# A hybrid decoder trunk: modulation products held back in pairs two to six of each group by tokens

## The chip, the core and the metric

One core of a Trainium2 chip. Its engines work side by side, each through a queue of its own in order: TensorE (PE, with PEld for the loading of its weights), VectorE (DVE), ScalarE (ACT), GpSimd (POOL) and SyncE (SP), which here only issues DMAs. The time is that of one execution on the device in microseconds (us), the median of several runs. Lower is better.

## The reference

Two layers, 256 tokens, a model width of 2048, all in float32. The modulation is `mod = silu(c) @ w_mod[i] + b_mod[i]`: 6 x 2048 numbers per layer from one vector `c`, so 12 x 8192 KB of weights a layer for very little arithmetic.

```python
c_act = jax.nn.silu(c)
for i in range(DEPTH):                      # 2 layers
    mod = (c_act @ w_mod[i] + b_mod[i])[:, None, :]
    sh1, sc1, g1, sh2, sc2, g2 = jnp.split(mod, 6, axis=-1)
    h = rms_norm(x, norm1_g[i]) * (1.0 + sc1) + sh1
    y = retention_mixer(h, ...) if i == 0 else short_conv_mixer(h, ...)
    x = x + g1 * y
    h = rms_norm(x, norm2_g[i]) * (1.0 + sc2) + sh2
    a, b = jnp.split(h @ ffn_w_in[i], 2, axis=-1)      # 2048 -> 2 x 5632
    x = x + g2 * ((silu(a) * b) @ ffn_w_out[i])        # 5632 -> 2048
return rms_norm(x, final_g)
```

## The kernel before

**Weights.** All weights of the products lie in `w_all`, in the order of their use, in chunks of 128 x 2048 numbers (1 MB). A chunk holds 16 blocks of 128 x 128, and it is loaded by `fetch` into one of three buffers named raw. `prepare` then splits it in pieces of 128 x 1024: ACT copies a piece to `hi` in a rounded format (line 395), DVE makes `lo = raw - hi` (line 398), and PE multiplies with both. There are four buffers each for hi and lo, and `take` prepares two pieces (three in parts of the feed-forward) ahead of the one in use.

**Modulation.** `modulation(layer, which, j)` makes 128 numbers of `mod`. It loads 1 MB of `w_mod` into a raw buffer of the same three, multiplies it on DVE with `cb` (silu of `c` on all partitions) and sums along the row in one instruction (line 311, 128 x 2048), and POOL adds the bias. There are 192 of these. 32 are made at the start; the other 160 are in the list `todo` in the order of their need: gate 1, scale 2, shift 2 and gate 2 of layer 0, then all six parts of layer 1. The instruction of line 311 has a low priority (`MOD_PRIO`) where the scheduler orders DVE's queue.

**When a modulation begins.** Every product calls `paced(n)` with the blocks that it used. `plan_mod` says how many modulations are due after so many blocks, and `allowed` grows by 0.045 a block up to 2.0, so `paced` begins at most one in about 22 blocks, or two at once when none was begun for a while. A call with more than 64 blocks sets `allowed` to zero. `needed(layer, which)` begins all that a step needs and that are not yet begun. One such call is `needed(1, GT2)` in line 1273, between the convolution and the last feed-forward: it empties `todo`, because the buffer of `cb` is used for something else from there.

**Groups by tokens.** In the feed-forward's input, `gathered` computes 128 + 128 tokens by 1024 columns (512 of each half of the SwiGLU) over all 16 blocks of rows, taken as eight pairs of rows, one chunk each. In an ordinary pair, a chunk takes 24 matmuls. Some pairs are of the class `Seven`: seven products in place of eight (Strassen-Winograd, 21 matmuls), for which DVE makes differences of the weights (lines 384 to 390) besides the lo's. Layer 0 has two pairs of seven in a group, the fourth and the sixth; layer 1 has three. After the last pair of seven, `mixed_sums` empties four banks (lines 1121 to 1125); after the group, line 1163 empties the other four. The results are multiplied and, at the third pair of the next group, transposed by PE (line 1177). Layer 0 has four groups in the first part and six in the second, each part followed by the feed-forward's output. Layer 1's output uses `gathered` too, when no modulation is left.

PE's order is written out by hand. The other engines' order comes from a scheduler in the recording layer, at build time.

Of the kernel before, what the change touches and what calls it, by code (L numbers as in the profile page):

```python
# [40 lines left out]
FIRST_SEVEN, IN_SEVEN, OUT_SEVEN, TURNS_AT, BESIDE_CB, BESIDE_SUMS = (3, 5), (3, 4, 6), ((2, 4, 6), (2, 4, 6)), 2, 40, 48  # L41
FFN_TILES = 20, 24
STORE_AT, LOAD_AT = 0, 2
LEAD_RET, LEAD_CONV, LEAD_FFN, TURN_ROW = 6, 4, 4, 6
AHEAD = 2
MOD_LEAD = 64
# [203 lines left out]
def trunk(ctx: ExitStack, tc: tile.TileContext, x_in, c_in, pos_in, w_mod, cols_in, gain_in, tab_in, w_all, out):  # L250
# [55 lines left out]
    def modulation(layer, which, j):  # L306
        t = layer * 6 * KT + which * KT + j
        raw = mod_raw(t)
        total = tmp("msum", (P, 1), bufs=4)
        with tc.high_priority(offset=MOD_PRIO):  # L310
            nc.vector.scalar_tensor_tensor(raw, raw, 1.0, cb, op0=ALU.mult, op1=ALU.mult, accum_out=total)  # L311
        b = b_mod[:, t : t + 1]
        norm = 0 if which < SH2 else 1
        if which in (SC1, SC2):
            m = tmp("mcol", (P, 1), bufs=4)
            nc.gpsimd.tensor_scalar(m, total, b, 1.0, op0=ALU.add, op1=ALU.add)
            dst = mod_a[layer][norm][:, j : j + 1]
            nc.gpsimd.tensor_tensor(dst, m, gain[norm][layer][:, j : j + 1], op=ALU.mult)
        else:
            dst = (mod_s if which in (SH1, SH2) else mod_g)[layer][norm][:, j : j + 1]  # L320
            nc.gpsimd.tensor_tensor(dst, total, b, op=ALU.add)

    todo = []
# [3 lines left out]
    n_mod = len(todo)  # L327
# [1 line left out]
    first = RET_SPANS[0].n * FIRST_KS  # L329
    early = sum(g.n * len(g.ks) for g in RET_SPANS)  # L330
    plan_mod = [(early, 0), (1024, 18), (1984, 49), (5184, n_mod)]
    units, allowed = [0], [0.0]

    def paced(n):

        units[0] += n
        due = 0
        for (a, i), (b, j) in zip(plan_mod, plan_mod[1:]):
            if units[0] >= a:
                due = min(j, i + (units[0] - a) * (j - i) // (b - a))  # L340
        allowed[0] = min(allowed[0] + n * MOST, 2.0) if n <= 64 else 0.0
        while todo and n_mod - len(todo) < due and allowed[0] >= 1.0:
            allowed[0] -= 1.0
            modulation(*todo.pop())

# [57 lines left out]
    def take(group, k, col, width=P):  # L403

        assert order.pop() == (group, k, col, width)
        i = place[0] or 0
        if i == 0:
            if place[0] == 0:
                ready.pop(0)
            while len(ready) < 1 + ahead_now[0] * (units[0] >= first):  # L410
                n = len(ready)
                prepare()
                if len(ready) == n:
                    break
        place[0] = (i + width) % ready[0][2]
        return [t[:, i : i + width] for t in ready[0][:2]]
# [13 lines left out]
    def product(g, act, base=0, before=None, banks=None, last=True):  # L430

        fresh = not banks
        banks = banks or [bank() for _ in g.cols]
        for k in g.ks:
            if before:
                before(k)
            h = act[k - base]
            for c, pt in zip(g.cols, banks):
                hi, lo = take(g, k, c)
                nc.tensor.matmul(  # L440
                    pt, hi, h, start=fresh and k == g.ks[0], stop=False, skip_group_check=True
                )
                nc.tensor.matmul(  # L443
                    pt[:, 1, :], lo, h[:, 0, :], start=False, stop=last and k == g.ks[-1], skip_group_check=True
                )
            ticked(len(g.cols))
        paced(len(g.cols) * len(g.ks))
        return banks
# [11 lines left out]
    def by_token(banks, hi, lo, h, first, last, halves=range(2)):  # L460

        for t in halves:
            thrice(banks[t], half_of(h, t), (hi, lo), first, last)

    def packed(g, act, base=0, before=None, between=None, banks=None):

        banks = banks or [bank() for _ in range((g.n + 1) // 2)]  # L470
        for k in g.ks:
            if before:
                before(k)
            h = act[k - base]
            at = 0
            for i, (c, width) in enumerate(g.items):
                if between and i == len(g.items) // 2:
                    between(k)
                hi, lo = take(g, k, c, width)
                if width == DV:  # L480
                    both = [v.rearrange("p a b -> p (a b)") for v in banks[at // 2 : at // 2 + 2]]
                    by_token(both, hi, lo, h, k == g.ks[0], k == g.ks[-1])
                    at += 4
                    continue
                pt = banks[at // 2][:, at % 2, :]
                first, last = k == g.ks[0] and at % 2 == 0, k == g.ks[-1]
                nc.tensor.matmul(pt, hi, h[:, 0, :], start=first, stop=False, skip_group_check=True)  # L487
                nc.tensor.matmul(pt, hi, h[:, 1, :], start=False, stop=False, skip_group_check=True)  # L488
                nc.tensor.matmul(pt, lo, h[:, 0, :], start=False, stop=last, skip_group_check=True)  # L489
                at += 1  # L490
            ticked(g.n)
        paced(g.n * len(g.ks))
        return banks
# [103 lines left out]
    def normed(accs, layer, norm, g):  # L597
# [18 lines left out]
        for k in g.ks:  # L616
# [11 lines left out]
            elif k > SPREAD_AT:  # L628
                more(min(k, made[0] + 2))
        more(KT)  # L630
        paced(len(g.cols) * len(g.ks))

        def total(pt, dst=None):
# [38 lines left out]
    with ExitStack() as inner:  # L672
# [64 lines left out]
        with tc.tile_pool(name="start", bufs=1) as sp:  # L737
# [132 lines left out]
            due, step = [], [0.0]  # L870
# [229 lines left out]
    def flat_bank():  # L1100
        return bank().rearrange("p a b -> p (a b)")

    def sevens(g, act, base, sums, ours, banks, first, last):

        s1, s2, s4 = [[v[:, n, :] for n in range(2)] for v in sums]
        (a11, s3), (a12, a22) = [[half_of(act[k - base], t) for t in range(2)] for k in g.ks]
        p1, p5, p6, p7 = [(b, first, last) for b in banks]
        for use, x, (o, a, z) in zip(g.uses(), (s4, a12, s1, s3, a11, s2, a22), (
            (ours[0, 1], False, False), (ours[0, 0], False, False), p5, p7, p1, p6, (ours[1, 0], False, False)
        )):  # L1110
            thrice(o, x, take(*use), a, z)
            if use[2] in ("B21", "T3", "T2"):
                paced(4)
        paced(4)

    def mixed_sums(banks):

        p1, p5, p6, p7 = banks
        u1, u3 = halves_of
        u2, u4 = [tmp("u512", (P, DV), pool=mpool, bufs=3) for _ in range(2)]  # L1120
        nc.scalar.copy(u1, p1)
        nc.vector.tensor_tensor(u2, p6, u1, op=ALU.add)
        nc.vector.tensor_tensor(u3, p7, u2, op=ALU.add)
        nc.vector.tensor_tensor(u4, p5, u3, op=ALU.add)
        nc.vector.tensor_tensor(u2, p5, u2, op=ALU.add)
        return {(0, 0): u1, (1, 0): u3, (1, 1): u4, (0, 1): u2}
# [3 lines left out]
    def gathered(groups, act, base, sums, beside=None, mixed=None, single=None):  # L1130

        ours = {(t, j): flat_bank() for t in range(2) for j in range(2)}
        banks, n = [], len(sums)
        for i, g in enumerate(groups):
            if beside:
                beside(i)
            if i == TURNS_AT and waiting:
                waiting.pop(0)()
            if isinstance(g, Seven):
                n -= 1  # L1140
                banks = banks or [flat_bank() for _ in range(4)]
                of = sums[(g.ks[0] - base) // 2]
                sevens(g, act, base, of, ours, banks, n == len(sums) - 1, n == 0)
                if not n:
                    extra = mixed_sums(banks)
                    if mixed:
                        mixed(extra)
                continue
            if len(g.cols) == 1:
                single(g, ours, g is groups[-1])  # L1150
                continue
            for k in g.ks:
                for j, item in enumerate(g.items):
                    ends = i == 0 and k == g.ks[0], g is groups[-1] and k == g.ks[-1]
                    by_token([ours[t, j] for t in range(2)], *take(g, k, *item), act[k - base], *ends)
                paced(g.n)
        return ours, extra
# [241 lines left out]
    for part in range(2):  # L1399
# [10 lines left out]
        for i, groups in enumerate(LAST_IN[part]):  # L1410
            due = OUT_SEVEN[part]
# [42 lines left out]
```

## Time and profile before

| | us |
|---|---|
| median of 3 runs | 2627.31 |
| lowest and highest | 2624.63, 2629.22 |
| the profiled execution, its own time | 2629.53 |
| its span, first to last instruction | 2627.8 |
| PE busy in the span | 2570.7 (98%) |
| DVE busy | 2296.9 (87%) |
| line 311 (modulation), 160 instructions on DVE | 365.9 |
| line 398 (lo) on 128 x 1024 from raw, 912 instructions on DVE | 1104.0 |
| DMA, mean over the span | 262 GB/s |
| granted TensorE clock, mean | 0.998 |

In rows of the timeline, the first number is the start in us from the span's start, the second the duration, then come engine, line, operation, out<-in and shapes; the bracket at the end is the engine's idle time ahead of it, with what ended it. In rows of the stretches, each engine has its busy time and its instructions, then come the granted clock, the DMA engines' busy share and GB/s.

### The profile page before, as it was taken

What the parts mean: (1) busy time and instruction counts of PE and PEld (TensorE: products, weight loads), DVE (VectorE), ACT (ScalarE), POOL (GpSimd) and SP (SyncE); (2) the same over time, 40 slices, a digit from 0 to 9 for tenths busy, and PEclk for the clock granted to TensorE, in tenths of its full rate; (3) what the DMA queues carried; (4) which work ended last, traced back from release to release, by engine and by line L of the source; (5) the groups of instructions that cost most, each with busy time, mean ns of one, the idle gap of its engine ahead of it and who ended that gap; (6) DMA issues with size and microseconds to landing.
All of it is one profiled execution on the core that took longest, in us unless ns stands there. A gap on an engine that the chain in (4) does not pass through costs nothing.

```text
span 2627.8 us, 35162 instructions
## 1 busy us (share of the span) xinstructions
PE 2570.7 (98%) x13563; PEld 2197.6 (84%) x13563; DVE 2296.9 (87%) x2838; ACT 1312.3 (50%) x1726; POOL 140.6 (5%) x232
## 2 busy tenths in 40 slices
PE   7999999999999999999999999999999999999998
PEld 6898889888898777877778899888898888888886
DVE  7988978887799998889998889988988998999978
ACT  5544543444456444334444455444565564565554
POOL 0000000010000011100000000000000000000000
PEclk9999999999999999999999999999999999999999
DMA  9976668777686776877777777887755555555653
GB/s 399 385 289 225 253 253 303 280 268 265 255 305 230 293 293 258 297 291 292 268 290 273 282 297 286 323 302 291 286 194 192 207 208 209 184 213 180 222 211 145
DMA packets 96683, 689.48 MB, mean 262 GB/s; under 512 B 10737, under 2 KB 12161, under 8 KB 13441
## 3 DMA queue, kind: packets, MB, share of 16 engines
q1 hardware_dynamic: 96514, 687.23, 70.3%
q8 instruction: 106, 1.74, 0.3%
q14 instruction: 63, 0.52, 0.1%
HBM read 685.08 MB, written 2.11 MB: 262 GB/s over the span
## 4 chain that ended last, share of the span: by engine, by line
PE 76%; DVE 14%; DMA 6%; issue 3%; ACT 1%; ACTq 0%; DVEq 0%; POOLq 0%; POOL 0%; SPq 0%
PE bank L440 17%; PE bank L454 13%; PE bank L455 13%; PE bank L453 13%; PE bank L443 9%; DVE lo L398 6%; DMA raw<-w_all 5%; DVE raw L311 2%; PE bank L489 2%; PE bank L488 2%; PE bank L487 2%; PE bank L620 1%; PE bank L622 1%; PE bank L621 1%; DMA raw<-w_mod 1%
## 5 line engine op out<-in xcount | busy, mean ns | idle before, releaser
L395 ACT CAST hi<-raw 128x1024 fp32r<-128x1024 f32 (+1 forms) x974 | 984.7, 1024 | 1036.6 <-PE bank L455 347.6
L398 DVE TENSOR_TENSOR lo<-raw,hi 128x1024 fp32r<-128x1024 f32 (+1 forms) x974 | 1143.4, 1188 | 242.7 <-ACT hi L395 237.8
L454 PE MATMUL bank<-lo,h 128*128 128x512 f32 x1592 | 628.3, 395 | 23.3 <-DVE lo L398 22.8
L453 PE MATMUL bank<-hi,h 128*128 128x512 f32 x1592 | 626.4, 393 | 3.2 <-DVE rm L732 2.4
L455 PE MATMUL bank<-hi,h 128*128 128x512 f32 x1592 | 622.4, 391 | 0.0
L454 PEld LDWEIGHTS bank<-lo,h 128*128 128x128 f32 x1592 | 300.2, 189 | 101.0 <-DVE lo L398 43.0
L311 DVE SCALAR_TENSOR_TENSOR raw<-raw,cb 128x2048 f32<-128x2048 f32 x160 | 365.9, 2287 | 19.4 <-DMA raw<-w_mod 18.3
L453 PEld LDWEIGHTS bank<-hi,h 128*128 128x128 f32 x1592 | 300.1, 188 | 67.5 <-ACT hi L395 4.5
L455 PEld LDWEIGHTS bank<-hi,h 128*128 128x128 f32 x1592 | 300.0, 188 | 61.8
L440 PE MATMUL bank<-mid,hi 128*128 128x512 f32 x920 | 319.6, 391 | 0.2 <-ACT hi L395 0.2
L443 PE MATMUL bank<-mid,lo 128*128 128x256 f32 x920 | 259.6, 282 | 2.3 <-DVE lo L398 2.3
L440 PE MATMUL bank<-h,hi 128*128 128x512 f32 x736 | 255.4, 391 | 0.0
L443 PE MATMUL bank<-h,lo 128*128 128x256 f32 x736 | 207.4, 282 | 0.0
L440 PEld LDWEIGHTS bank<-mid,hi 128*128 128x128 f32 x920 | 172.6, 188 | 36.2 <-ACT hi L395 0.5
L443 PEld LDWEIGHTS bank<-mid,lo 128*128 128x128 f32 x920 | 174.1, 189 | 3.1 <-DVE lo L398 3.0
L440 PE MATMUL bank<-rm,hi 128*128 128x512 f32 x496 | 172.5, 391 | 0.0
L440 PEld LDWEIGHTS bank<-h,hi 128*128 128x128 f32 x736 | 138.1, 188 | 28.8
L489 PE MATMUL bank<-h,lo 128*128 128x256 f32 x512 | 146.3, 286 | 4.8 <-DVE lo L398 4.8
L487 PE MATMUL bank<-h,hi 128*128 128x256 f32 x512 | 145.6, 284 | 3.3 <-ACT h L776 3.3
L488 PE MATMUL bank<-h,hi 128*128 128x256 f32 x512 | 145.6, 284 | 0.7 <-DVE h L777 0.7
L443 PE MATMUL bank<-rm,lo 128*128 128x256 f32 x496 | 139.9, 282 | 0.0
L443 PEld LDWEIGHTS bank<-h,lo 128*128 128x128 f32 x736 | 139.3, 189 | 0.0
(273 smaller groups left out, 3430.2 us busy)
## 6 DMA issues: line engine op xcount, KB each, us to landing
raw<-w_all SPq DMA_DIRECT2D x456, 1024.0 KB, 4.9
raw<-w_mod SPq DMA_DIRECT2D x192, 1024.0 KB, 5.6
x<-x_in SPq DMA_DIRECT2D x4, 512.0 KB, 5.4
out<-xt SPq DMA_DIRECT2D x4, 512.0 KB, 3.0
decay<-tab_in SPq DMA_DIRECT2D x8, 128.0 KB, 2.3
x<-gate_row SPq DMA_DIRECT2D x2, 512.0 KB, 4.3
last_gain<-gain_in SPq DMA_DIRECT2D x1, 1024.0 KB, 7.2
cols<-cols_in SPq DMA_DIRECT2D x1, 152.0 KB, 8.7
```

Of the source, the lines that this page charges most:

```text
L311: nc.vector.scalar_tensor_tensor(raw, raw, 1.0, cb, op0=ALU.mult, op1=ALU.mult, accum_out=total)
L395: nc.scalar.copy(hi, raw)
L398: nc.vector.tensor_tensor(lo, raw, hi.bitcast(F32), op=ALU.subtract)
L440: nc.tensor.matmul(pt, hi, h, start=fresh and k == g.ks[0], stop=False, skip_group_check=True)
L443: nc.tensor.matmul(pt[:, 1, :], lo, h[:, 0, :], start=False, stop=last and k == g.ks[-1], skip_group_check=True)
L453: nc.tensor.matmul(o, hi, w_hi, start=first, stop=False)
L454: nc.tensor.matmul(o, hi, w_lo, start=False, stop=False)
L455: nc.tensor.matmul(o, lo, w_hi, start=False, stop=last)
L487: nc.tensor.matmul(pt, hi, h[:, 0, :], start=first, stop=False, skip_group_check=True)
L488: nc.tensor.matmul(pt, hi, h[:, 1, :], start=False, stop=False, skip_group_check=True)
L489: nc.tensor.matmul(pt, lo, h[:, 0, :], start=False, stop=last, skip_group_check=True)
L620: nc.tensor.matmul(pt, hi, high, start=k == 0, stop=False, skip_group_check=True)
```

## The change

`paced` begins no modulation while `hold[0]` is set, and `gathered` sets it for the pairs 1 to 5 of a group, counted from zero. `allowed` still grows in these pairs, up to its cap. At the seventh pair two modulations may begin at once, and `needed` is as it was.

```diff
+HELD = range(1, 6)
...
-    units, allowed = [0], [0.0]
+    units, allowed, hold = [0], [0.0], [False]
...
         allowed[0] = min(allowed[0] + n * MOST, 2.0) if n <= 64 else 0.0
-        while todo and n_mod - len(todo) < due and allowed[0] >= 1.0:
+        while todo and n_mod - len(todo) < due and allowed[0] >= 1.0 and not hold[0]:
             allowed[0] -= 1.0
             modulation(*todo.pop())
...
         for i, g in enumerate(groups):
             if beside:
                 beside(i)
+            hold[0] = i in HELD
             if i == TURNS_AT and waiting:
                 waiting.pop(0)()
```

PE's order is the same in both kernels. Lines from 44 on stand one or two lines later in the changed kernel (lo is line 399 there, the modulation 312). The order of the instructions on DVE, in the second group of layer 0's first part, from the last piece of the fourth pair (a pair of seven) to the sixth pair. Before:

```order
L398 TENSOR_TENSOR lo_8412<-raw_8335,hi_8411 128x512
L311 SCALAR_TENSOR_TENSOR raw_8401,msum_8403<-raw_8401,cb 128x2048
L398 TENSOR_TENSOR lo_8424<-raw_8421,hi_8423 128x1024
L398 TENSOR_TENSOR lo_8434<-raw_8421,hi_8433 128x1024
L384 TENSOR_TENSOR differences<-raw_8443 128x1024
L398 TENSOR_TENSOR lo_8447<-raw_8443,hi_8446 128x1024
```

In the changed kernel, at the same place:

```order
L399 TENSOR_TENSOR lo_8392<-raw_8320,hi_8391 128x512
L399 TENSOR_TENSOR lo_8404<-raw_8401,hi_8403 128x1024
L399 TENSOR_TENSOR lo_8414<-raw_8401,hi_8413 128x1024
L399 TENSOR_TENSOR lo_8427<-raw_8423,hi_8426 128x1024
L399 TENSOR_TENSOR lo_8434<-differences,hi_8433 128x1024
```

The modulation behind the pair of seven is gone, and the difference for the sixth pair is made earlier (ahead of these rows).

DVE again, from the seventh pair's second lo to the first two lo's of the next group, in the changed kernel. The operations on bank are those that empty the products of seven (lines 1123 to 1126) and the first of the group's other banks (line 1165):

```order
L399 TENSOR_TENSOR lo_8490<-raw_8477,hi_8489 128x1024
L1123 TENSOR_TENSOR u_1548_8508<-bank_8388,halves 128x512
L399 TENSOR_TENSOR lo_8502<-raw_8499,hi_8501 128x1024
L1124 TENSOR_TENSOR halves<-bank_8389,u_1548_8508 128x512
L399 TENSOR_TENSOR lo_8516<-raw_8499,hi_8515 128x1024
L1125 TENSOR_TENSOR u_1549_8509<-bank_8387,halves 128x512
L1126 TENSOR_TENSOR u_1548_8508<-bank_8387,u_1548_8508 128x512
L312 SCALAR_TENSOR_TENSOR raw_8531,msum_8533<-raw_8531,cb 128x2048
L312 SCALAR_TENSOR_TENSOR raw_8536,msum_8538<-raw_8536,cb 128x2048
L1165 TENSOR_TENSOR halves<-bank_8266,halves 128x512
L399 TENSOR_TENSOR lo_8544<-raw_8541,hi_8543 128x1024
L399 TENSOR_TENSOR lo_8560<-raw_8541,hi_8559 128x1024
```

Before, one modulation stands between the lo's of the seventh pair and the sums, and one among the sums. Now two stand in a row behind the sums, and the next group's first lo comes behind the first operation that empties the group's banks.

The third place is the end of the convolution, on DVE: from the lo of the last layer's first chunk past the last evacuation of the convolution's output (line 657, or 658) to the lo of the second chunk. Before:

```order
L398 TENSOR_TENSOR lo_17308<-raw_17277,hi_17307 128x1024
L665 SCALAR_TENSOR_TENSOR x_76<-bank_17220,g_91,sum_17268 128x256
L311 SCALAR_TENSOR_TENSOR raw_17335,msum_17337<-raw_17335,cb 128x2048
L515 TENSOR_TENSOR acc_16651<-acc_16651,sq_17271 128x256
L595 SCALAR_TENSOR_TENSOR h<-x_76,a_84,h 128x256
L657 SCALAR_TENSOR_TENSOR x_76<-bank_17276,g_91,x_76 128x256
L398 TENSOR_TENSOR lo_17382<-raw_17379,hi_17381 128x1024
```

In the changed kernel:

```order
L399 TENSOR_TENSOR lo_17238<-raw_17207,hi_17237 128x1024
L658 SCALAR_TENSOR_TENSOR x_76<-bank_17206,g_91,x_76 128x256
L312 SCALAR_TENSOR_TENSOR raw_17291,msum_17293<-raw_17291,cb 128x2048
L596 SCALAR_TENSOR_TENSOR h<-x_76,a_84,h 128x256
L312 SCALAR_TENSOR_TENSOR raw_17296,msum_17298<-raw_17296,cb 128x2048
L538 TENSOR_SCALAR rs_17430<-bank_17425 128x2
L312 SCALAR_TENSOR_TENSOR raw_17301,msum_17303<-raw_17301,cb 128x2048
...
L312 SCALAR_TENSOR_TENSOR raw_17361,msum_17363<-raw_17361,cb 128x2048
L399 TENSOR_TENSOR lo_17382<-raw_17379,hi_17381 128x1024
```

The dots leave out eleven more of line 312: 15 stand between the two lo's, where one stood ahead of the last evacuation. On SP, the 15 loads of `w_mod` stand in a row as well, ahead of the load of the second chunk.

## The prediction

> **What bounds the kernel now.** I read the page first, then the busy time by stretch, then the times of equal work in two layers, then the timeline at one stall.
>
> ```profile
> span 2627.8 us, 35162 instructions
> PE 2570.7 (98%) x13563; PEld 2197.6 (84%) x13563; DVE 2296.9 (87%) x2838; ACT 1312.3 (50%) x1726; POOL 140.6 (5%) x232
> L395 ACT CAST hi<-raw 128x1024 fp32r<-128x1024 f32 (+1 forms) x974 | 984.7, 1024 | 1036.6 <-PE bank L455 347.6
> ```
>
> PE seems full. The stages differ, though. In the timeline below, each row is the eight transposes that PE makes at the third pair of a group by tokens (of the group before). The first two rows are two groups apart in the first part of layer 0, the next two are five groups apart in its second part, and the last two are four groups apart in layer 1, where nothing of the modulation is left.
>
> ```profile
> 882.95 1.04 PE L1177 MATMUL bank<-tab,halves 128*128 128x128 f32 x8
> 982.32 1.04 PE L1177 MATMUL bank<-tab,halves 128*128 128x128 f32 x8
> 1194.61 1.03 PE L1177 MATMUL bank<-tab,halves 128*128 128x128 f32 x8
> 1424.33 1.04 PE L1177 MATMUL bank<-tab,halves 128*128 128x128 f32 x8
> 2288.48 1.03 PE L1177 MATMUL bank<-tab,x 128*128 128x128 f32 x8
> 2458.88 1.03 PE L1177 MATMUL bank<-tab,x 128*128 128x128 f32 x8
> ```
>
> A group takes 99.37/2 = 49.7 us, 229.72/5 = 45.9 us and 170.40/4 = 42.6 us. A layer-1 group has three pairs of seven products: 5 x 24 + 3 x 21 + 8 = 191 matmuls. A layer-0 group has two: 194. At layer 1's pace a layer-0 group would take 42.6 x 194/191 = 43.3 us. So layer 0 loses 6.4 us in each of four groups and 2.6 us in each of six: 25.6 + 15.6 = 41 us. That is the most this stage can give.
>
> The busy time in the same three stretches, and in one of the convolution's input, all engines and then the modulation's line alone:
>
> ```profile
> core 0: us, PE busy (x) PEld busy (x) DVE busy (x) ACT busy (x) POOL busy (x), PEclk, DMA share, GB/s
> 882.90:982.30 99.40, 91.09 (x389) 70.42 (x388) 92.91 (x100) 44.15 (x50) 13.85 (x16) 1.00 0.79 293
> 1194.60:1424.30 229.70, 221.32 (x971) 175.35 (x970) 216.69 (x231) 111.08 (x126) 15.97 (x21) 1.00 0.74 279
> 2288.50:2458.90 170.40, 170.40 (x766) 140.42 (x765) 158.57 (x191) 99.89 (x117) 0.00 (x0) 1.00 0.55 197
> 1480.00:1640.00 160.00, 160.00 (x1043) 146.94 (x1042) 144.00 (x203) 79.86 (x122) 15.04 (x31) 1.00 0.80 297
> ...
> 882.90:982.30 99.40, 27.55 (x24) 1.00 0.79 293
> 1194.60:1424.30 229.70, 50.21 (x43) 1.00 0.74 279
> ```
>
> DVE is 93% and 94% busy where PE loses time. Without the modulation it would need (92.91 - 27.55)/2 = 32.7 us a group, or (216.69 - 50.21)/5 = 33.3. A modulation is 27.55/12 = 2.30 us. So DVE sets the pace there, and PE's gaps show only part of it: 8.3 us in the first stretch and 8.4 in the second, by group 4 x 4.15 + 6 x 1.68 = 27 us over the ten. [...]
>
> One stall, in the timeline, DVE and PE:
>
> ```profile
> 889.61 0.68 DVE L388 TENSOR_TENSOR raw<-raw,differences 128x512 f32<-128x512 f32 x1
> 890.21 1.22 DVE L398 TENSOR_TENSOR lo<-differences,hi 128x1024 fp32r<-128x1024 f32 x1
> 891.35 0.69 DVE L390 TENSOR_TENSOR raw<-raw 128x512 f32<-128x512 f32 x1
> 891.95 1.82 DVE L398 TENSOR_TENSOR lo<-raw,hi 128x1024 fp32r<-128x1024 f32 x2
> 893.69 2.29 DVE L311 SCALAR_TENSOR_TENSOR raw<-raw,cb 128x2048 f32<-128x2048 f32 x1
> 895.90 2.36 DVE L398 TENSOR_TENSOR lo<-raw,hi 128x1024 fp32r<-128x1024 f32 x2
> 897.17 0.50 PE L454 MATMUL bank<-lo,h 128*128 128x512 f32 x1 [1.60 <-DVE lo L398]
> ```
>
> From start to start, DVE's queue moves on by 0.60 us for an operation on 512 columns, 1.14 for a lo and 2.21 for a modulation. The modulation of 893.69 stands right behind a pair of seven and ahead of the fifth pair's lo. PE waits 1.60 us for that lo.
>
> **The change, part by part.** All 160 modulations of L311 stay. By the two orders, the ten groups of layer 0 hold 49 of them before and 30 after (three each). Of the 19, three go to the convolution's input, two to its output, and 14 to its end, where 15 now stand together instead of one, because the call needed(1, GT2) of line 1273 forces whatever is left.
>
> *What goes.* With three modulations a group needs 33.3 + 3 x 2.3 = 40.2 us of DVE in 43.3: 93%. That is the share of the third stretch (158.57 of 170.40), where PE is busy for all of 170.40. So the floor can be reached. What may be late next is the group's end, where two modulations now follow one another. Let T be PE's end of the sixth pair. The lo of the seventh pair's second piece needs its hi, whose buffer comes free nine matmuls (9 x 0.23 = 2.1 us) before T. The hi takes 1.02 us and the lo 1.22, so it ends at T + 0.1. Behind it DVE has two lo's and four operations on 512 columns (4.7 us), two modulations (4.4), one operation that empties a bank (0.6), and then the next group's first lo (1.2): T + 11.0. PE wants it after 48 matmuls and one more, at T + 11.0 by the layer-1 pace (42.6/191 = 0.223 us) or T + 11.3 by 0.23. I take 0.3 us a group, 3 us in all. The ends are 0 and the 1.60 of the row above, 16 us. Gain: 41 - 3 = 38 us, between 25 and 41. Below nothing is excluded, since the stage holds 19 fewer modulations and nothing new.
>
> *What is added in the convolution.* Five modulations more run at a pace that the convolution's input already has in its first half. There PE is busy for 160.00 of 160 us while DVE is at 144.00. I take 0. Without that cover it is 5 x 2.3 = 11.5.
>
> *The 15 in a row.* The rows around the convolution's end: DVE, PE (first matmuls of the last layer's first group), DMA around 1870 us, then DMA near the start.
>
> ```profile
> 1904.46 0.48 DVE L664 SCALAR_TENSOR_TENSOR sum<-bank,g,x 128x256 f32<-128x256 f32 x1
> 1906.38 2.28 DVE L311 SCALAR_TENSOR_TENSOR raw<-raw,cb 128x2048 f32<-128x2048 f32 x1
> 1909.33 0.48 DVE L657 SCALAR_TENSOR_TENSOR x<-bank,g,x 128x256 f32<-128x256 f32 x1
> 1910.64 1.23 DVE L398 TENSOR_TENSOR lo<-raw,hi 128x1024 fp32r<-128x1024 f32 x1 [0.83 <-ACT hi L395]
> 1909.07 0.28 PE L620 MATMUL bank<-h,hi 128*128 128x258 f32 x1
> 1909.43 0.28 PE L620 MATMUL bank<-h,hi 128*128 128x258 f32 x1
> raw<-w_all SPq DMA_DIRECT2D x4, 1024.0 KB, 5.0
> raw<-w_mod SPq DMA_DIRECT2D x1, 1024.0 KB, 5.0
> DMA packets 885, 5.48 MB, mean 422 GB/s; under 512 B 96, under 2 KB 224, under 8 KB 224
> ```
>
> Behind the 15 stand the lo's of every later weight, and on SP the DMA of the next weights, so PE has only two pieces of eight blocks: 16 x 0.36 = 5.8 us, until 1909.07 + 5.8 = 1914.8. DVE comes to the 15 at about 1911.2: from 1904.46 it still has one modulation, two lo's and five short operations, 2.2 + 2 x 1.14 + 5 x 0.45 = 6.7. The raw ring has three buffers. A modulation's buffer is reloaded when it is done, so three take 2.3 + 5.0 + 0.15 = 7.45 us, or 2.5 each; 1.05 MB at 422 GB/s is 2.5 too. The first three are spaced alike, so the last ends at about 1911.2 + 15 x 2.5 = 1948.7. The next weights take the buffer of the 13th, free at 1943.7, and land at 1948.7. The hi then ends at 1949.7 and the lo at 1950.9. PE loses 1950.9 - 1914.9 = 36 us. At DVE's own 2.3 a modulation it would be 33; at the page's 5.6 to landing of all w_mod loads (below), 2.7 each and 39.
>
> ```profile
> raw<-w_mod SPq DMA_DIRECT2D x192, 1024.0 KB, 5.6
> 20.22 0.58 PE L488 MATMUL bank<-h,hi 128*128 128x256 f32 x1 [0.51 <-DVE h L777]
> 24.01 0.63 PE L453 MATMUL bank<-hi,h 128*128 128x512 f32 x1
> 24.44 0.63 PE L454 MATMUL bank<-lo,h 128*128 128x512 f32 x1
> 28.23 0.40 PE L454 MATMUL bank<-lo,h 128*128 128x512 f32 x1
> 28.46 0.39 PE L455 MATMUL bank<-hi,h 128*128 128x512 f32 x1
> ```
>
> After its pauses at the start, PE began dense work at 20.22 and still went at 0.43 a matmul at 24.44, against 0.23 at 28.23: half clock for 4 us or more, so about 2 us lost. I add 2 for the idle time of 36 us; the ends are 0 and 3. [...] No run here shows it behind so long an idle time. The burst: 38 us, between 33 and 42.
>
> *Sum.* The profiled execution took 2629.53 us, 2.2 over the median 2627.31. 2629.5 - 38 + 38 = 2629.5. The two terms cancel, and what is left, nothing within some 8 us, is smaller than their bounds.
>
> **The rivals.** *Slower, at the group's end.* If the next group's first lo comes 1.6 us late instead of 0.3, ten groups give back 13 us more: 2642. It decides from about 0.65 us a group. For it: the walk above has no slack. Against it: the layer-1 groups keep PE full at the same share of DVE. Chance 0.24. *Slower, since PE's gaps are all there is to win.* Then the gain is 27 - 3 = 24 and the time 2643. Equal matmuls in 42.6 us speak against it: 0.08. *Faster.* The groups reach the floor (41) and the burst goes at DVE's pace without the clock's loss (33): 2629.5 - 41 + 33 = 2621.5. For it: DVE's share of 93%. Against it: the ring of three and 5.0 us a load. Chance 0.22. That the change leaves the order as it was is excluded by the orders.
>
> **How the numbers follow.** A measurement of this kernel can tell about 0.2% (5.3 us) from no change. My forecast, the cancelling, has 0.46 and its own range is 2623 to 2635. Its middle gives 2630, rounded up since the slower cases reach further. Faster than 2622.1 is the fast rival without its nearer end: 0.18. Slower than 2632.6 takes both slow rivals and some of the forecast's upper end: 0.36. Within: 0.46. The range of 2619 to 2643 leaves out the far ends of the rivals.
>
> **What would show it.** Right: groups of layer 0 at about 43.3 to 43.9 us between the transposes, three L311 each, no PE wait behind a pair of seven; 15 L311 in a row on DVE with about 2.5 us from one to the next; one PE wait of about 36 us there, and a granted clock below 1 just behind it. Wrong: groups at 45 us, with PE waiting for the lo at a group's first matmuls; L311 in the row at 2.2 us or at 3; or a burst that PE outlasts.

## The result, and the profile after

The changed kernel takes 2634.54 us (median of 20 runs, 2626.74 to 2642.48), the kernel before 2627.68 in the same comparison (20 runs, 2623.57 to 2636.62): ratio 1.0025, 95% interval 1.0015 to 1.0035. That is 6.9 us slower, just past the 0.2% that a measurement tells from no change. The forecast of 2630 had the two large terms cancel. They are there, with nearly the forecast sizes, and the loss is the larger by some 5 us. The profiled execution took 2635.04 us.

From the page after, and then the one row of the page before that answers to its last line (PE's matmul on lo; the number before the arrow is PE's idle time there):

```profile
span 2633.3 us, 35134 instructions
PE 2560.3 (97%) x13563; PEld 2200.0 (84%) x13563; DVE 2297.7 (87%) x2838; ACT 1307.8 (50%) x1726; POOL 135.4 (5%) x232
L455 PE MATMUL bank<-lo,h 128*128 128x512 f32 x1592 | 623.9, 392 | 4.6 <-DVE lo L399 4.0
```

```profile
L454 PE MATMUL bank<-lo,h 128*128 128x512 f32 x1592 | 628.3, 395 | 23.3 <-DVE lo L398 22.8
```

DVE does the same work as before. PE's waits for lo have gone from 22.8 to 4.0 us, and the span is longer all the same. The transposes of after (timeline), at the markers that the prediction used, and the first of layer 1 in both kernels, after and then before:

```profile
878.63 1.04 PE L1179 MATMUL bank<-tab,halves 128*128 128x128 f32 x8
968.79 1.04 PE L1179 MATMUL bank<-tab,halves 128*128 128x128 f32 x8
1168.43 1.04 PE L1179 MATMUL bank<-tab,halves 128*128 128x128 f32 x8
1387.42 1.04 PE L1179 MATMUL bank<-tab,halves 128*128 128x128 f32 x8
2017.41 1.03 PE L1179 MATMUL bank<-tab,x 128*128 128x128 f32 x8
```

```profile
2012.05 1.03 PE L1177 MATMUL bank<-tab,x 128*128 128x128 f32 x8
```

| stretch | before | after | difference |
|---|---|---|---|
| start to the first marker | 882.95 | 878.63 | -4.3 |
| two groups of the first part | 99.37 | 90.16 | -9.2 |
| from there over the output to the second part | 212.29 | 199.64 | -12.7 |
| five groups of the second part | 229.72 | 218.99 | -10.7 |
| the convolution, to layer 1's first marker | 587.72 | 629.99 | +42.3 |

Gain 36.9 us up to the last marker of layer 0, loss 42.3 in the convolution, 5.4 us together; the spans differ by 5.5. From layer 1's first marker to the end both take the same. Of the gain, 35.7 us lie in the ten groups, 20.3 in the first part and 15.4 in the second. Layer 0's first output, which lies in the third stretch of the table, takes 103.5 us in both kernels, from the last transposes of the first part to the first matmul of the second (timeline, before and then after):

```profile
1032.81 1.04 PE L1177 MATMUL bank<-tab,halves 128*128 128x128 f32 x8
...
1136.30 0.39 PE L453 MATMUL bank<-hi,h 128*128 128x512 f32 x1
```

```profile
1011.27 1.04 PE L1179 MATMUL bank<-tab,halves 128*128 128x128 f32 x8
...
1114.76 0.39 PE L454 MATMUL bank<-hi,h 128*128 128x512 f32 x1
```

The stretches of after, all engines, then line 312 alone (each modulation counts as two instructions):

```profile
878.63:968.79 90.16, 88.27 (x389) 71.01 (x388) 81.74 (x89) 43.62 (x50) 6.95 (x6) 1.00 0.69 257
1168.43:1387.42 218.99, 216.26 (x971) 176.47 (x970) 202.03 (x218) 109.13 (x125) 18.42 (x19) 1.00 0.70 260
```

```profile
878.63:968.79 90.16, 13.59 (x12) 1.00 0.69 257
1168.43:1387.42 218.99, 33.60 (x29) 1.00 0.70 260
```

PE is now idle for 1.9 and 2.7 us in them (8.3 and 8.4 before), and DVE is at 91 and 92%. Two of the waits that are left, each at the first lo of a group, with two modulations ahead of it on DVE:

```profile
1201.98 0.50 PE L455 MATMUL bank<-lo,h 128*128 128x512 f32 x1 [0.40 <-DVE lo L399]
...
1290.93 0.50 PE L455 MATMUL bank<-lo,h 128*128 128x512 f32 x1 [0.28 <-DVE lo L399]
```

The row of 15 modulations at the convolution's end: the timeline of DVE, DVE's group over 1876 to 1917 us (busy, mean ns, idle before), the DMA issues of 1876 to 1912, and PE's and ACT's timelines behind the row:

```profile
1876.10 2.28 DVE L312 SCALAR_TENSOR_TENSOR raw<-raw,cb 128x2048 f32<-128x2048 f32 x1
...
1885.88 2.29 DVE L312 SCALAR_TENSOR_TENSOR raw<-raw,cb 128x2048 f32<-128x2048 f32 x1 [0.19 <-DMA raw<-w_mod]
...
1903.96 2.29 DVE L312 SCALAR_TENSOR_TENSOR raw<-raw,cb 128x2048 f32<-128x2048 f32 x1 [1.62 <-DMA raw<-w_mod]
...
1914.24 2.29 DVE L312 SCALAR_TENSOR_TENSOR raw<-raw,cb 128x2048 f32<-128x2048 f32 x1
```

```profile
L312 DVE SCALAR_TENSOR_TENSOR raw<-raw,cb 128x2048 f32<-128x2048 f32 x15 | 34.4, 2290 | 5.7 <-DMA raw<-w_mod 5.4
```

```profile
raw<-w_mod SPq DMA_DIRECT2D x13, 1024.0 KB, 5.4
```

```profile
1917.87 0.58 PE L621 MATMUL bank<-h,hi 128*128 128x258 f32 x1 [37.45 <-ACT hi L396]
...
1919.13 0.58 PE L623 MATMUL bank<-h,lo 128*128 128x258 f32 x1 [0.47 <-DVE lo L399]
```

```profile
1916.77 1.99 ACT L396 CAST hi<-raw 128x1024 fp32r<-128x1024 f32 x2 [39.73 <-DMA raw<-w_all]
```

The 15 go from 1876.10 to 1916.5, 40.4 us, 2.69 each, and DVE waits 5.4 us among them for the loads. PE stands still for 37.45 us. It names ACT's hi, which waits for the weights' load, which waits for a raw buffer behind the modulations (SP's waits from 1870 to 1920 us: 6.6 us in three ahead of the weights' loads, for DVE's L312).

### The profile page after: what moved, and what is told of

It is laid out like the page before. It is cut to its first block, busy times and chain, and to the rows that moved or that the text cites. A ratio compares the mean times of both kernels' runs of the same rounds, so it can differ in the third digit from the quotient of the medians.

```text
span 2633.3 us, 35134 instructions
## 1 busy us (share of the span) xinstructions
PE 2560.3 (97%) x13563; PEld 2200.0 (84%) x13563; DVE 2297.7 (87%) x2838; ACT 1307.8 (50%) x1726; POOL 135.4 (5%) x232
## 4 chain that ended last, share of the span: by engine, by line
PE 82%; DVE 8%; DMA 5%; issue 2%; ACT 1%; ACTq 0%; DVEq 0%; POOLq 0%; POOL 0%; SPq 0%
PE bank L441 18%; PE bank L455 14%; PE bank L456 14%; PE bank L454 14%; PE bank L444 10%; DMA raw<-w_all 4%; DVE lo L399 3%; PE bank L490 2%; PE bank L489 2%; PE bank L488 2%; DMA raw<-w_mod 1%; PE bank L623 1%; PE bank L621 1%; PE bank L622 1%; ACT hi L396 1%
## 5 line engine op out<-in xcount | busy, mean ns | idle before, releaser
L312 DVE SCALAR_TENSOR_TENSOR raw<-raw,cb 128x2048 f32<-128x2048 f32 x160 | 364.8, 2285 | 17.6 <-DMA raw<-w_mod 17.2
```

## The experiments

**My theory.** A stretch takes PE's own time or DVE's sum, whichever is longer, so what counts in a group is the *number* of modulations; and the row costs by its length, as far as it outlasts PE's cover. **Rivals.** (1) What counts is the *place*: a modulation behind a pair of seven stops PE (the stall of the prediction), and elsewhere it is free. (2) What the convolution loses is not the row's doing. (3) The row's cost can't be had back: modulations moved out of it cost as much where they go. Medians and ratios are against the kernel before, run in the same series.

**The row taken away.** In the changed kernel, the 15 modulations that are left at the end are not made: part of gate 2 of layer 1 is zero.

```diff
-    needed(1, GT2)
+    while todo:
+        layer, which, j = todo.pop()
+        nc.gpsimd.memset(mod_g[layer][1][:, j : j + 1], 0.0)
```

> The changed kernel, but the 15 modulations that stand in a row at the convolution's end aren't made (their gates are set to zero, so this part of the computation is left out). Nothing else moves. Theory (the gain of the groups and the price of the row cancel): the row and the half clock behind it go, about 41 us, so about 2593 us against 2634 of the changed kernel and 2628 of before. Rival (the time went into the groups' ends, or into the clock alone): the time falls by a few us at most beyond the 15 x 2.3 us of VectorE that nobody waits for, to 2625 or more.

2593.13 us, ratio 0.9872 (0.9856 to 0.9889). The transposes (timeline):

```profile
878.71 1.04 PE L1179 MATMUL bank<-tab,halves 128*128 128x128 f32 x8
...
1384.13 1.04 PE L1179 MATMUL bank<-tab,halves 128*128 128x128 f32 x8
1970.88 1.03 PE L1179 MATMUL bank<-tab,x 128*128 128x128 f32 x8
```

The convolution's stretch is 586.75 us instead of 629.99. The row costs 2634.5 - 2593.1 = 41.4 us by the medians, and the rest of the change gains 34.5 against 2627.7. Rival 2 falls.

**The row alone.** The kernel before, with its last 15 kept back and no pairs held:

```diff
+        due = min(due, n_mod - 15)
```

> The kernel before, with no hold in the groups, but with the last 15 modulations kept back until the same place at the convolution's end. Theory: the groups stay at 49.7 and 45.9 us, and the row alone costs 41 us: about 2668 us. Rival: if the row is partly hidden by what TensorE has in hand, or if the changed kernel lost its time elsewhere, it costs 20 us or less: 2648 or less.

2660.09 us, 1.0119 (1.0102 to 1.0136): +32, where 41 was expected. In its order on DVE, three of the 15 stand ahead of the convolution's last evacuation and only 12 behind. A shorter row:

**Nine in the row.** The changed kernel with a faster pace early on, so that nine are left:

```diff
-    plan_mod = [(early, 0), (1024, 18), (1984, 49), (5184, n_mod)]
+    plan_mod = [(early, 0), (1024, 18), (1984, 63), (5184, n_mod)]
...
-        allowed[0] = min(allowed[0] + n * MOST, 2.0) if n <= 64 else 0.0
+        allowed[0] = min(allowed[0] + n * (0.06 if units[0] < 2048 else MOST), 2.0) if n <= 64 else 0.0
```

> As the changed kernel, with 0.06 a block in the retention: by the order 7 modulations more are made there (less 1 behind it) and 9 stand in the row at the convolution's end in place of 15. If the row's price goes by its length (2.7 us from one to the next, as the changed kernel's trace has it), it falls by 6 x 2.7 = 16 us, to 39 + 3 - 16 = 26 us above the 2593 without a row: about 2619 us. If it is a fixed price (the idle time begins anyway, and the clock falls), the time stays at 2630 or more.

2620.45 us, 0.9970 (0.9958 to 0.9981), as by length. PE's wait at the convolution's end (waits: us in total, times, longest) in the row alone, then with nine:

```profile
PE bank L621 <- ACT hi L396: 29.4, 1, 29.4
```

```profile
PE bank L621 <- ACT hi L396: 20.5, 1, 20.5
```

15, 12 and 9 behind PE's cover give 37.5, 29.4 and 20.5 us: 2.8 us for each one more. A kernel below with three in the row waits 2.9, one with two not at all for hi. Over these rows the price is a line in the length that begins at two.

**Only the first part held.**

```diff
-            hold[0] = i in HELD
+            hold[0] = i in HELD and units[0] < 2688
```

> The changed kernel with the hold in layer 0's first four groups alone. By the order these hold 3 modulations each in place of 5.5, the six groups of the second part 34 in all in place of 27, and the row at the convolution's end is one, as before. Theory (pace set by VectorE's work): the first part wins 4 x 6 = about 23 us, the second loses 7 x 2.3 = 16 us: about 2620 us. Rival (only the place counts, and the second part's groups stay as before): 2604 us.

2630.13 us, 1.0009 (0.9998 to 1.0020), worse than either expectation. The row of 15 is gone, since the modulations held back in the first part were made in the second: five or six stand in each of its groups, which take 47.5 to 54.4 us between transposes. The row's 42 us were paid there almost in full.

**A narrower hold.** `HELD = range(3, 6)`, in the changed kernel:

> The changed kernel with the hold from the fourth to the sixth pair alone (the two pairs of seven and the one between them). By the order the ten groups then hold 49 modulations, as many as before, four or five each, and none stands in a row at the convolution's end. If only the number of modulations counts (VectorE's work sets the pace), the groups stay at about 47.4 us on the mean, and the time is that of before, 2625 to 2630 us. If the place counts too (a modulation behind a pair of seven stalls TensorE, elsewhere it fits), VectorE needs 33.3 + 4.9 x 2.3 = 44.6 us a group and the groups take about 45 us: 2627 - 24 = about 2604 us.

2614.77 us, 0.9957 (0.9942 to 0.9972), between the two. Four to six a group, 44.7 to 46.9 us between transposes. The ten groups hold as many modulations as in the kernel before, and it is 13 us faster: at this number, the place counts too, though not for all of the time.

**Earlier, to empty the row.** The changed kernel with 0.09 a block up to block 2048 and (1984, 66) in the plan; the same in the kernel before, without the hold; and with `HELD = range(3, 6)`.

> The changed kernel, with the pace of the modulations raised from 0.045 to 0.09 a block in the retention and 66 of them due at its end in place of 49. By the order 64 are made there in place of 48, the groups keep 3 each, and none stands in a row at the convolution's end. Theory: the groups' gain stays and the row's price is gone, as when the row was left out (2593 us), with 0 to 7 us more for 16 modulations in the retention, where VectorE was 80 to 86% busy and TensorE full: 2593 to 2600 us. Rival: VectorE's work costs its full time there too, 16 x 2.3 = 37 us: 2630 us.

> The kernel before, without a hold, with the raised pace in the retention. By the order the ten groups hold 41 modulations (before: 49), at any pair, and there is no row. At 2.3 us for each of the 8 that went, 2628 - 18 = 2610 us.

> As the one without a hold and with the raised pace, but with the hold from the fourth to the sixth pair alone. By the order the ten groups hold 41 modulations, as many as there, and only their places differ. If the place counts, as the run with 49 and this hold suggested (2615 in place of 2628 us), about 13 us less than without a hold: 2597 us, no lower than 2593. If only the number counts, the same time as without a hold, 2610 us.

2614.71 (0.9949, 0.9934 to 0.9964), 2626.46 (1.0002, 0.9990 to 1.0014) and 2622.30 us (0.9987, 0.9974 to 1.0001), 12 to 25 us over my expectations. I had taken the stretch of 700 to 830 us (the retention's second output) as free. All engines and line 312 alone there, in the first of the three and then in the changed kernel:

```profile
700.00:830.00 130.00, 117.77 (x733) 106.42 (x732) 114.69 (x163) 58.63 (x89) 7.63 (x18) 0.95 0.74 274
...
700.00:830.00 130.00, 34.33 (x30) 0.95 0.74 274
```

```profile
700.00:830.00 130.00, 130.00 (x857) 119.62 (x856) 118.05 (x190) 76.18 (x131) 4.29 (x10) 1.00 0.68 251
...
700.00:830.00 130.00, 20.65 (x18) 1.00 0.68 251
```

Without the modulations, DVE needs 118.05 - 20.65 = 97.4 us for what PE does there in 130. With 15 modulations that makes 131.7: no room, and PE did 733 matmuls instead of 857. It is the same sum as in the groups, which I had not made for this stretch. It isn't the whole price: DVE was busy for 114.69 of the 130 us, not for all of them, and the granted clock was 0.95. The last two kernels hold the same number at other places and differ by 4 us, within their intervals: that settles nothing.

**Spread out.** So the next one begins most of them earlier, where DVE has room, and more in the convolution's input:

```diff
-    plan_mod = [(early, 0), (1024, 18), (1984, 49), (5184, n_mod)]
+    plan_mod = [(early, 0), (1024, 18), (1984, 72), (5184, n_mod)]
...
-        allowed[0] = min(allowed[0] + n * MOST, 2.0) if n <= 64 else 0.0
+        allowed[0] = min(allowed[0] + n * (0.12 if units[0] < 1792 else 0.05 if 4160 <= units[0] < 4928 else MOST), 2.0) if n <= 64 else 0.0
```

> The changed kernel, with the modulations of the row begun earlier and farther apart than in the two earlier tries: the pace is 0.12 a block up to block 1792 (feed-forward input and output before the second retention's output are over by then), 0.05 in the blocks 4160 to 4928, and the plan is (1984, 72). 58 are begun before layer 0's groups, 30 in them, 33 in the convolution's input, and 2 are left for the row at the convolution's end. The theory, that the price of a modulation is set by what its place leaves idle, on DVE and in the raw ring, and that the row's price is its length: groups as in the changed kernel (43 to 45 us each), 0 to 5 us more before the groups, a row of 2 lies behind PE's cover of 5.8 us and costs under 2 us, so 2594 to 2600 us. The rival, that any work moved out of the row costs elsewhere about what it saves, as in the try with a faster pace whose 700 to 830 us lost 17 us: 2612 us or more.

2596.42 us, 0.9876 (0.9856 to 0.9896): faster than both kernels, with every modulation made, and within 3.3 us of the one that left 15 out. Rival 3, which held for the first part's modulations, isn't a rule. Its page, and its transposes at the ends of the second part and the convolution:

```profile
span 2594.7 us, 35137 instructions
PE 2558.0 (99%) x13563; PEld 2197.6 (85%) x13563; DVE 2295.5 (88%) x2838; ACT 1307.8 (50%) x1726; POOL 141.7 (5%) x232
```

```profile
1168.73 1.03 PE L1179 MATMUL bank<-tab,halves 128*128 128x128 f32 x8
...
1386.79 1.04 PE L1179 MATMUL bank<-tab,halves 128*128 128x128 f32 x8
1979.58 1.03 PE L1179 MATMUL bank<-tab,x 128*128 128x128 f32 x8
```

Five groups in 218.1 us as in the changed kernel, and the convolution in 592.8: 37 us of the row's price are gone, and 6 are left, 4 of them in short waits of PE.

**Four in a group.** The same early pace, no faster pace in the convolution, `HELD = range(2, 6)`:

> The same faster pace up to block 1792 and the same plan, without the faster pace in the convolution, and with the pairs held back being 2 to 5 in place of 1 to 5, so that four modulations fit into most groups of layer 0: 58 are begun before the groups, 39 in them and 1 is left for the row. 9 more in the groups than in the kernel with the wider hold. If one more in a group costs 1.5 to 2.5 us, as the kernels before (49 in the groups) and with the hold in the pairs 3 to 5 show between them: 13 to 23 us more than the run with 30, so 2607 to 2620. If four in a group are hidden as three are: 2594 to 2600.

2601.55 us, 0.9889 (0.9865 to 0.9913). Eight more in the eight intervals that I count (32 against 24) take 8.0 us more: 1.0 each, less than expected.

**Number or place.** As the spread kernel, but a group's modulations begin at the two pairs of seven alone, with the hold taken off at a group's end:

```diff
-HELD = range(1, 6)
+HELD = (0, 1, 2, 4, 6, 7)
...
                 paced(g.n)
+        hold[0] = False
```

> The kernel with the early pace and the plan (1984, 72) that has 3 modulations in each group and 2 in the row, with one difference: in a group, modulations are begun at the two pairs of seven alone (the fourth and the sixth), where they were begun outside the pairs 2 to 6. The numbers stay: 31 in the groups (30 there), 33 in the convolution's input, 3 in the row (2). By number alone, 3 of 2.3 us beside 33.3 us of DVE's other work fit into 43.3 us, so 2594 to 2602 us, with groups at 43 to 45. By place, a modulation behind a pair of seven makes PE wait as in the profile of before (1.6 us at one of them), two or three such in each of 10 groups: groups of 45 to 48 us, 15 to 40 us more in all, 2612 to 2636.

2604.84 us, 0.9921 (0.9906 to 0.9935). Its DVE in the first part (timeline), PE's waits from 880 to 1440 us (us in total, times, longest), and two of its transposes, four groups apart:

```profile
946.18 1.82 DVE L399 TENSOR_TENSOR lo<-raw,hi 128x1024 fp32r<-128x1024 f32 x2
947.92 2.28 DVE L312 SCALAR_TENSOR_TENSOR raw<-raw,cb 128x2048 f32<-128x2048 f32 x1
...
950.13 2.35 DVE L399 TENSOR_TENSOR lo<-raw,hi 128x1024 fp32r<-128x1024 f32 x2
```

```profile
PE bank L455 <- DVE lo L399: 3.1, 4, 1.4
```

```profile
1174.82 1.04 PE L1180 MATMUL bank<-tab,halves 128*128 128x128 f32 x8
...
1348.29 1.03 PE L1180 MATMUL bank<-tab,halves 128*128 128x128 f32 x8
```

The modulation stands behind a pair of seven and ahead of the next pair's two lo's, as in the stall of the prediction. A group takes 173.47/4 = 43.4 us, which is PE's own time. So with three a group, this place costs nothing, and rival 1 falls there. The time is 2.8 us over the range by number and 7 under the range by place. By the profiles this kernel is 6.8 us over the spread kernel: 1.8 us more ahead of the feed-forward's input, 2.3 and 3.6 from the first matmul of each part to its first transposes, 4.2 in the convolution with a row of three, and 4.9 less between the transposes. In the first part's first stretch both kernels have four modulations, so that the 2.3 us go with the place; in the second part's it is four against three. PE's waits from 1014 to 1175 us, where the spread kernel has none in that first stretch:

```profile
PE bank L455 <- DVE lo L399: 2.8, 3, 1.4
```

Over the ten groups together this place costs 1.1 us, where 15 to 40 were expected by place.

**Nothing held.** The spread kernel with `HELD = ()`:

> The same early pace and plan with nothing held back: 48 modulations in layer 0's groups instead of 30 (5 or 6 in most of them), 21 in the convolution's input, 1 in the row. By DVE's sum, 33.3 us and 2.3 for each, a group of 5 takes 44.8 and one of 6 takes 47.1 at least, where 3 take 43.3. By number alone (these floors): about 15 us more than with the hold, 2611. If place counts too, as the kernel before's groups of 46 to 50 us say (49.7 and 45.9 on the mean): 25 to 40 us more, 2620 to 2636. If the early pace is what made the good kernel, and not the hold: within 5 us of 2596.

2640.92 us, 1.0059 (1.0041 to 1.0077): 44.5 more than with the hold, above the dearest case expected. The pace alone doesn't make the good kernel. One of its groups of six, all engines:

```profile
1197.80:1253.80 56.00, 48.97 (x196) 37.57 (x195) 47.66 (x51) 22.28 (x26) 4.27 (x6) 0.94 0.70 265
```

DVE is busy for 47.66 us, its sum for six (33.3 + 6 x 2.3 = 47.1), but the group takes 56.0.

Over all 14 profiles, six intervals of 194 matmuls from transposes to transposes in each (without the last of each part, which goes over into other work and is shorter):

| modulations in the interval | intervals | mean us (lowest to highest) | DVE's sum, 33.3 + 2.3 each |
|---|---|---|---|
| 3 | 41 | 44.1 (43.3 to 47.0) | 40.2 |
| 4 | 20 | 45.2 (43.3 to 46.2) | 42.5 |
| 5 | 10 | 47.7 (46.5 to 50.2) | 44.8 |
| 6 | 13 | 50.2 (46.5 to 56.0) | 47.1 |

Up to four, PE's 43.3 us is the larger and the mean interval is within 2 us of it; from four on each one more adds 2.5 on the mean, near DVE's price of one, 2.3. So the number decides whether a group has room, by DVE's sum. Where it has none, the place counts too. The five intervals with five or six in the two kernels with `HELD = range(3, 6)` took 46.5 to 46.9 us, near DVE's sum; in the kernels that hold no pair of these groups, five took 46.5 to 50.2 and six 48.6 to 56.0. For five and six, rival 1 therefore stands beside the theory: the narrower hold shows 13 us at the same number, and how the place costs them is not shown. Part of what lies over DVE's sum goes with the clock (last section): the mean granted clock was 0.94 in the longest interval, 56.0 us, and 0.97 in that of 52.4, and it was at half for 6.8 us in that of 54.4 and for 3.4 in that of 50.2. In the group of 56.0 us, DVE also waited 5.6 us for ACT's hi, and I have no run that separates this.

## Why the prediction came out as it did

- *The groups would fall to 43.3 to 43.9 us.* They fell to 45.1 and 43.8 us, and the gain up to the last marker is 36.9 against 38. Right in size, and not quite in its parts: the groups of the first part give 20.3 us where 25.6 were worked out, since they kept 1.8 us over the floor, and the stretch from the part's first matmul to its first transposes gained only 3.1 us; those of the second part give 15.4 against 15.6. The first part's 45.1 us is nearer to the prediction's own sign of being wrong (45) than to that of being right.
- *PE's gaps or equal work.* The gaps' 27 us would have been wrong. PEld's busy share of the first stretch goes the same way: 71% before (70.42 of 99.40), 79% after (71.01 of 90.16), against 82% in layer 1 (140.42 of 170.40).
- *The next wait is at a group's end, 0.3 us.* The wait is there, of about that size, at the first lo of two groups (0.40 and 0.28 us), and at the other groups' ends it isn't. So 3 us for all ten was too much for this term. Of the 4.0 us of lo waits that are left from 880 to 1440 us, 3.0 stand inside the fourth pair, a pair of seven, which the steps hadn't counted. The slower rival of 1.6 us a group fails.
- *The stall at 893.69 stands for the cause.* With three a group it is not the cause: the same sequence on DVE lets PE run on. The step from DVE's 93% was the right one. With five or six in a group, as before the change, the runs leave a share of the loss to the place.
- *Five more in the convolution cost nothing.* In the kernel without the row, the convolution takes 586.75 us, 1 less than before. Right.
- *The row: 2.5 us each, PE loses 36.* The mechanism is as worked out, the ring of three raw buffers included, and only its size is off: 2.69 each, since a load took 5.4 us instead of the 5.0 of a row with one load. (2.3 + 5.4 + 0.15)/3 gives 2.62, where the 0.15 is my estimate; I have not broken out the rest. 15 x 0.19 is 2.9 us. PE lost 37.45 + 0.47. With 2.6 for the clock (below) that is 40.5 of the 42.3 us; the rest are short waits, 0.31 and 0.75 of them just ahead of the row. This is the term that was mis-sized: 42.3 instead of 38, 0.3 past its bound of 42.
- *The clock: 2 us.* This was my estimate from PE's pace at the start of the kernel before, and no run had shown it behind so long an idle time. Behind the 37.45 us it was 2.6 (last section).
- *The sum.* -38 + 38 became -36.9 + 42.3. The forecast was the cancelling, and this is the cancelling with the burst at its upper end; 2634.5 lies in the range and in its own range of 2623 to 2635, but the difference is just past 0.2%. The most likely case, no difference beyond 0.2% (0.46), did not come; a slower kernel had 0.36. The two misses, 1.1 and 4.3 us, point the same way and make up the 5.4. In the first term there was some luck: the 3 us set aside for the groups' ends were mostly not lost there, and they covered part of the 5.3 us by which the first part fell short.

## What to carry to other kernels

To place filler work on an engine, add up that engine's time per stretch beside PE's: while the sum stayed under PE's time here, filler cost little (nothing for three in a group, about 1 us for the fourth), and past that each piece cost about its whole length on the mean (2.5 us against DVE's 2.3), more or less by the place where it stood. Work that is held back must have a place to go: what a due time forced into one row here cost its length, less PE's cover (37.45 us of PE's wait for 15), with the next weights' loads queued behind it. The same hold was 0.25% slower with the row and 1.2% faster once the held work was begun earlier, and without the hold the same early start was 0.6% slower.

## What the hardware showed

The granted clock was at half from 1882.7 to 1923.7 us here, from 1922.3 to 1953.0 with the row alone and from 1890.6 to 1911.1 with nine: 41.0, 30.7 and 20.5 us. The half clock in the second fence below lasted 3.4 us; the three are about 12, 9 and 6 times that. Stretches of after, around the fall and the return (all engines, the clock third from last):

```profile
1875.90:1879.30 3.40, 3.40 (x31) 3.40 (x30) 3.40 (x5) 0.82 (x2) 0.37 (x1) 1.00 0.70 243
1879.30:1882.70 3.40, 1.12 (x10) 0.91 (x8) 3.40 (x4) 0.00 (x0) 1.62 (x1) 1.00 1.00 395
1916.90:1920.30 3.40, 1.97 (x7) 1.67 (x8) 2.36 (x2) 2.92 (x4) 0.00 (x0) 0.50 1.00 419
1920.30:1923.70 3.40, 3.40 (x18) 3.40 (x17) 2.36 (x2) 0.94 (x1) 0.00 (x0) 0.50 0.83 275
1923.70:1927.10 3.40, 3.40 (x31) 3.40 (x31) 2.18 (x4) 2.53 (x5) 0.00 (x0) 1.00 0.95 381
```

And in the kernel with nothing held, in a group, where PE's waits around the fall were of 0.63 to 1.69 us:

```profile
1208.90:1212.30 3.40, 1.83 (x6) 1.05 (x6) 3.40 (x5) 0.62 (x1) 0.59 (x1) 1.00 0.81 289
1212.30:1215.70 3.40, 1.40 (x4) 0.65 (x5) 2.00 (x3) 1.99 (x2) 0.57 (x1) 1.00 0.63 241
1215.70:1219.10 3.40, 3.40 (x9) 2.64 (x10) 2.86 (x3) 1.66 (x2) 0.00 (x0) 0.50 1.05 434
```

A stretch in which PE was busy for 1.83 of 3.40 us was followed by full clock; one with 1.40, 59% idle in three waits of 0.63 to 1.59 us, was followed by half clock, and so was the one with 1.12 in the changed kernel. There the clock was back at full behind a stretch that was full of work (3.40 of 3.40), and stayed at half behind the one with 1.97. PE resumed at 1917.87 and got the full clock at 1923.7, 5.8 us later, after 23 matmuls in 5.4 us of work. At full clock they go at 0.12 us each (1925.15 to 1925.27), 2.8 in all: 2.6 us lost.
